# A decoder trunk's first norm: x read a second time by tokens for its square sums, first weights in three pieces, second pair in own buffers

## The chip, the cores and the metric

One core of a Trainium2 chip runs the whole program in one launch. The metric is the device time of one execution in microseconds (us). Kernel before: median 1245.22 us of 3 runs (1245.1 to 1245.67).

## The reference

A trunk of two layers on x of 512 tokens by 1024 features, all in float32. The first step of the first layer is the only part that the change touches:

```
u = x * rsqrt(mean(x*x, over features) + EPS) * conv_norm_g
a = u @ w_pw1 + b_pw1                       # 1024 -> 2048
c = a[:, :1024] * sigmoid(a[:, 1024:])
c = causal depthwise convolution over 31 tokens + dw_b
c = silu(layer_norm(c)) @ w_pw2 + b_pw2
h = x + c
```

Behind it come a SwiGLU block, a gated input embedding, and a second layer with differential attention.

## The kernel before, in words

Activations lie transposed: features on the 128 partitions, the 512 tokens along the free dimension, so x is eight chunks `h[0..7]` of 128x512. Every float32 operand of a large product is cut into an upper and a lower part of reduced precision (ScalarE casts the upper part, VectorE subtracts it from the original), and a product is three matmuls of 128x512 (`mm3`, L165 to L169): lower by upper, upper by upper, upper by lower.

The first step works in chunks c = 0..7 of the output. Each has two weights of 128x1024, one for the gate and one for the value (a pair): 24 matmuls for each of the two. The per-token factor rsqrt(...) is not applied to the input but to the products: `norm.split` (L215) scales a chunk of x by the gain alone and cuts it; the factor comes as a tile `rb` of 128x512 with the same row on each partition, and VectorE multiplies gate and value by it (L567, L573) when they are read from PSUM. So products can start before the factor is known, but nothing behind them can.

The factor is formed so: the squares of the eight chunks (L317, ScalarE) are summed over the features. Chunks 0, 1 and 2 go alone to TensorE and chunks 3 to 7 are first added by GpSimd into one tile (L319); TensorE sums each over its partitions by four matmuls with a matrix of ones (`columns_sum`, L198). VectorE scales the four columns (L262), GpSimd takes the power -0.5 (L264), VectorE spreads the result on a diagonal (L269), TensorE multiplies it by ones (`spread`, L282), and ScalarE copies it to `rb` (L254).

Weights arrive through two buffers `wraw` by DMAs of SyncE's queue (SP in the profile); upper parts have four buffers `whi`, lower parts four `wlo`, so two pairs are in flight. The first pair, weights w0 (gate) and w1 (value), comes in two halves each, between the loads of x; in this prologue the order on ScalarE and VectorE is written out by hand (L327), everything else is ordered by a scheduler. The second pair, w2 and w3, is loaded by `weight` (L148) when `wraw` is free.

After the products, each chunk goes through the 31 taps of the convolution. Chunks 0, 2, 4 and 7 use VectorE (L496, a multiply-add per tap) and GpSimd (L484); chunk 7 also uses TensorE. Chunks 1, 3, 5 and 6 are "phased": the gated product (L579) is written to DRAM (`pi`, L408), read back rearranged (`C<-pi`, L412), multiplied by tap matrices on TensorE (36 matmuls of 128x128, L445), copied by ScalarE (L453), written to DRAM (`po`, L455) and read back (`B<-po`, L458), and VectorE adds the bias (L463). Where a chunk's TensorE taps stand between the products is fixed by `BETWEEN` and `BEHIND` (L62) and the scheduler. The layer norm behind the taps needs the column sums of all chunks (L198 again), a variance (L631 to L633, L262, L264), a diagonal by ScalarE (L641) and its product (L644); products that depend on nothing there (`factor`, L598) fill TensorE meanwhile.

Of the kernel before, what the change touches and what calls it, by code (L numbers as in the profile page):

```python
# [13 lines left out]
F32R = mybir.dt.float32r  # L14
AF = mybir.ActivationFunctionType
ALU = mybir.AluOpType
# [4 lines left out]
P = 128  # L21
S = 512
D = 1024
NC = D // P
# [64 lines left out]


@with_exitstack
def trunk(ctx, tc, xT, pT, wts, diag, dww, vec, rel, onehot, lamv, out):
    nc = tc.nc
    V, A, G, T = nc.vector, nc.scalar, nc.gpsimd, nc.tensor

# [98 lines left out]
    def columns_sum(t, src, first, last):  # L194

        for b in range(4):
            cut = slice(b * P, (b + 1) * P)
            r = T.matmul(t[:, cut], src[:, cut], ones, start=first and b == 0, stop=last and b == 3)  # L198
        return r

    def first_of(t):
        return t.rearrange("p (b k) -> p b k", b=4)[:, :, 0]
# [5 lines left out]
    class Norm:  # L208
# [51 lines left out]
    def rsqrt_cols(src, n, inv):  # L260
        v = sb([P, P // 2], "v8", 2)[:, :8]
        last_v[0] = V.tensor_scalar(v[:, :n], src, inv, EPS, ALU.mult, ALU.add)  # L262
        r = sb([P, P // 2], "r8", 2)[:, :8]
        last_pow[0] = G.tensor_tensor(r[:, :n], v[:, :n], mhalf[:, :n], ALU.pow)  # L264
        return r[:, :n]
# [21 lines left out]


    norm = Norm("conv_g")
    wnext[0] = 2  # L290
    raw2 = [sb([P, 1024], "wraw", 2) for _ in range(2)]
    w0, w1 = ([sb([P, 1024], t, 4, F32R) for t in ("whi", "wlo")] for _ in range(2))
    pieces = ((slice(0, S), slice(S, 1024)),) * 2

    def load(c):
        nc.sync.dma_start(h[c], xT[c])

    def fetch(i, k):
        return nc.sync.dma_start(raw2[i][:, pieces[i][k]], wts[i, :, pieces[i][k]])

    fetch(0, 0)
    load(0)
    load(1)
    fetch(1, 0)
    load(2)
    fetch(0, 1)
    load(3)
    pair_loads = [fetch(1, 1)]
    pairs = [(w1, w0)]
    for c in range(4, NC):  # L310
        load(c)

    squares = {}

    def square(c):
        sq = squares[c] = wk() if c != 3 else sb([P, S], "acc", 1)
        A.activation(sq, h[c], AF.Square)  # L317
        if c > 3:
            G.tensor_tensor(squares[3], squares[3], sq, ALU.add)  # L319

    def first_split(i, k):
        hi, lo = (w0, w1)[i]
        cut = pieces[i][k]
        A.copy(hi[:, cut], raw2[i][:, cut])
        V.tensor_tensor(lo[:, cut], raw2[i][:, cut], f(hi[:, cut]), ALU.subtract)

    with tc.manual_schedule(engines={V.engine, A.engine}):  # L327
        first_split(0, 0)
        norm.split(0)
        square(0)  # L330
        norm.split(1)
        first_split(1, 0)
        norm.split(2)
        first_split(0, 1)
        norm.split(3)
        first_split(1, 1)
        square(1)
        norm.split(4)
        square(3)
        for c in (5, 6, 7):  # L340
            norm.split(c)
            square(c - 1)
        square(7)
        square(2)

    def pfeatures(layer, parts):
        for k, (hi, lo) in enumerate(parts):
# [26 lines left out]
    last_sum = [None]  # L374
    rb = None

    def half(w, behind=None, start=0):
        acc = mm()
        for k in range(NC):
            with tc.issue_after(behind.ins) if behind and k >= start else nullcontext():  # L380
                mm3(acc, wpart(w, k), norm.u[k], k == 0, k == NC - 1)
        return acc

    def wt(c, j):
# [153 lines left out]
    for c in range(NC):  # L538
        wa, wg = pairs[c]
        if c == 0:  # L540
            pg, pa = mm(), mm()
            for k in range(NC):
                mm3(pg, wpart(wg, k), norm.u[k], k == 0, k == NC - 1)
                (ah, al), (bh, bl) = wpart(wa, k), norm.u[k]
                T.matmul(pa, ah, bh, start=k == 0, stop=False)
                T.matmul(pa, ah, bl, start=False, stop=False)
                T.matmul(pa, al, bh, start=False, stop=k == NC - 1)
            norm.dg = diagonal(norm.columns_of_chunks(squares))
            rb = norm.rows()
        if c + 1 < NC:  # L550
            late = ((first_gate, None), (first_gate, last_rows[0])) if c == 1 else ((None, None),) * 2
            pairs.append(tuple(weight(after=i) for i in late)[::-1])
            pair_loads.append(loaded[0])
        if c == 0:
            dwt = sb([P, NC * KW], "C4", 2)
            nc.sync.dma_start(dwt, dww)
        if c == 1:
            ph = pfeatures(0, [(sb([P, S], t, 2, F32R), sb([P, S], t, 2, F32R)) for t in ("wth", "wtl")])
        if c > 0:
            pg = half(wg, last_spread[0] if c == 1 else None, 6)  # L560
            for k in BETWEEN[c]:
                pe_taps(k)
            pa = half(wa, last_spread[0] if c == 1 else None)
# [12 lines left out]
        if c in PHASED:  # L576
            up = big()
            phases, tok = "p (r n) -> p n r", "p (n r) -> p n r"
            V.scalar_tensor_tensor(  # L579
                up.rearrange(phases, r=NPH), ta.rearrange(tok, r=NPH), col("b_pw1", c),  # L580
                tg.rearrange(tok, r=NPH), ALU.add, ALU.mult,
            )
# [771 lines left out]
def _layout(a):  # L1354
# [61 lines left out]
    def chunks(v):  # L1416
# [9 lines left out]
    cols = [chunks(vecs[n]) for n in VEC]  # L1426
    return {
        "xT": a["x"][0].T.reshape(NC, P, S),
        "pT": a["p"][:, 0].transpose(0, 2, 1).reshape(2, 2, P, S).transpose(0, 2, 1, 3).reshape(2, P, 2 * S),
        "wts": np.stack(tiles),  # L1430
        "diag": diag,
# [24 lines left out]
```

## Time and profile before

| | us |
|---|---|
| median of 3 runs | 1245.22 |
| the profiled execution, its own time | 1245.23 |
| its span in the profile | 1243.4 |
| TensorE matmul busy in the span | 1232.1 |
| VectorE, ScalarE, GpSimd busy | 882.0, 624.1, 469.8 |

The span begins with the first recorded instruction and lies 1.83 us below the execution's own time. Busy time of TensorE is modelled and overlaps from one matmul to the next, so small waits don't show in it; where matmuls start is the better reading. All times in rows are counted from the span's start. In a timeline row stand start, length, engine, line, operation, output and inputs, count, and in brackets the idle time before it and what ended it. PE is TensorE, PEld its weight load, DVE VectorE, ACT ScalarE, POOL GpSimd, SP SyncE, and SPq and ACTq are their queues that issue DMAs. A row of a stretch gives the stretch, its length, each engine's busy time, the granted clock, the DMA engines' share and GB/s. "in_wts" are weights, "in_xT" is x by features.

### The profile page before, as it was taken

How to read it: one execution, taken by the hardware profiler on the slowest of the kernel's cores; microseconds unless marked ns; L12 is line 12 of the kernel's file. 1: busy time of each engine (PE TensorE's matmuls, PEld its weight loads, DVE VectorE, ACT ScalarE, POOL GpSimd, SP SyncE). 2: the span in 40 equal slices, each digit the busy share in tenths (PEclk: the TensorE clock that was granted, in tenths of full speed). 3: DMA queues.
4: the chain of work that ended last, by engine and by line, in shares of the span. 5: the costliest groups of instructions: out<-in, count | busy, mean ns of one | idle time of the engine just before them, and what ended most of it. 6: DMA issues, size and time to landing. Idle time of an engine off the chain costs nothing.

```text
span 1243.4 us, 18433 instructions
## 1 busy us (share of the span) xinstructions
PE 1232.1 (99%) x7080; PEld 1080.6 (87%) x7080; DVE 882.0 (71%) x1242; ACT 624.1 (50%) x1096; POOL 469.8 (38%) x355
## 2 busy tenths in 40 slices
PE   9999999999999999999999999999999999999998
PEld 7888788888998899888888888788889998999887
DVE  6997866985895489547676876647966885588535
ACT  6652464433553255435566877735434552455432
POOL 2863432024670464133436635041026650562220
PEclk9999999999999999999999999999999999999999
DMA  7666224234333322334432330142332333232321
GB/s 255 199 212 187 85 55 125 88 99 126 88 100 119 103 86 77 110 104 153 127 111 76 107 101 28 52 152 86 90 126 91 102 114 111 82 103 89 102 99 68
DMA packets 49155, 136.34 MB, mean 110 GB/s; under 512 B 5635, under 2 KB 10243, under 8 KB 49068
## 3 DMA queue, kind: packets, MB, share of 16 engines
q1 hardware_dynamic: 46944, 131.74, 34.2%
q10 hardware_dynamic: 2124, 3.43, 1.0%
q8 instruction: 55, 0.90, 0.3%
q14 instruction: 32, 0.26, 0.1%
HBM read 128.84 MB, written 6.31 MB: 109 GB/s over the span
## 4 chain that ended last, share of the span: by engine, by line
PE 85%; DVE 7%; DMA 3%; issue 2%; ACT 1%; POOL 1%; SPq 1%; DVEq 0%; ACTq 0%; POOLq 0%
PE mm L167 27%; PE mm L168 27%; PE mm L169 27%; DVE sc L496 3%; PE mm L1172 1%; DVE wlo L162 1%; PE sc L1140 1%; PE sc L1139 1%; PE tp L1159 1%; PE tp L1093 1%; DMA B<-po 1%; DMA h<-in_xT 0%; PE tp L198 0%; DMA pi<-big 0%; DMA C<-pi 0%
## 5 line engine op out<-in xcount | busy, mean ns | idle before, releaser
L160 ACT CAST whi<-wraw 128x1024 fp32r<-128x1024 f32 (+1 forms) x141 | 143.5, 1025 | 232.0 <-PE mm L169 115.2
L162 DVE TENSOR_TENSOR wlo<-wraw,whi 128x1024 fp32r<-128x1024 f32 (+1 forms) x137 | 179.3, 1315 | 81.4 <-ACT whi L160 81.0
L167 PE MATMUL mm<-A,wlo 128*128 128x512 f32 (+1 forms) x560 | 218.0, 389 | 0.1
L168 PE MATMUL mm<-A,whi 128*128 128x512 f32 (+1 forms) x560 | 216.7, 387 | 0.0
L169 PE MATMUL mm<-A,whi 128*128 128x512 f32 (+1 forms) x560 | 213.3, 387 | 0.0
L167 PE MATMUL mm<-B,wlo 128*128 128x512 f32 x352 | 137.0, 389 | 0.0
L168 PE MATMUL mm<-B,whi 128*128 128x512 f32 x352 | 137.0, 389 | 0.0
L169 PE MATMUL mm<-B,whi 128*128 128x512 f32 x352 | 135.6, 389 | 0.0
L228 POOL TENSOR_TENSOR acc<-acc,wk 128x512 f32<-128x512 f32 x35 | 60.4, 1726 | 191.2 <-ACT wk L227 190.6
L168 PE MATMUL mm<-C,whi 128*128 128x256 f32 x448 | 126.8, 283 | 0.0
L169 PE MATMUL mm<-C,whi 128*128 128x256 f32 x448 | 126.8, 283 | 0.0
L167 PE MATMUL mm<-C,wlo 128*128 128x256 f32 x448 | 126.8, 283 | 0.0
L167 PEld LDWEIGHTS mm<-A,wlo 128*128 128x128 f32 x560 | 105.2, 188 | 22.1 <-DVE h L1303 0.5
L168 PEld LDWEIGHTS mm<-A,whi 128*128 128x128 f32 x560 | 105.2, 188 | 21.2 <-issue 0.5
L169 PEld LDWEIGHTS mm<-A,whi 128*128 128x128 f32 x560 | 105.2, 188 | 21.0
L766 DVE TENSOR_TENSOR wlo<-A,whi 128x1024 fp32r<-128x1024 f32 x60 | 108.2, 1814 | 19.3 <-ACT whi L765 19.3
L765 ACT CAST whi<-A 128x1024 fp32r<-128x1024 f32 x60 | 62.9, 1048 | 55.1 <-PE mm L169 44.0
L775 POOL TENSOR_TENSOR A<-wraw 128x512 f32<-128x512 f32 x16 | 25.1, 1569 | 168.5 <-DMA wraw<-in_wts 147.2
L775 POOL TENSOR_TENSOR A<-A 128x512 f32<-128x512 f32 x16 | 25.1, 1571 | 164.5 <-DMA A<-in_wts 155.6
L168 PEld LDWEIGHTS mm<-C,whi 128*128 128x128 f32 x448 | 86.0, 192 | 0.2
L167 PEld LDWEIGHTS mm<-C,wlo 128*128 128x128 f32 x448 | 86.0, 192 | 0.2
L169 PEld LDWEIGHTS mm<-C,whi 128*128 128x128 f32 x448 | 86.0, 192 | 0.0
(322 smaller groups left out, 3045.3 us busy)
## 6 DMA issues: line engine op xcount, KB each, us to landing
wraw<-in_wts SPq DMA_DIRECT2D x161, 512.0 KB, 3.6
A<-in_wts SPq DMA_DIRECT2D x32, 512.0 KB, 3.6
wraw<-in_wts SPq DMA_DIRECT2D x16, 384.0 KB, 3.1
D<-in_diag SPq DMA_DIRECT2D x22, 256.0 KB, 5.4
C<-in_diag SPq DMA_DIRECT2D x16, 256.0 KB, 5.1
h<-in_xT SPq DMA_DIRECT2D x8, 256.0 KB, 5.6
rest<-h SPq DMA_DIRECT2D x8, 256.0 KB, 3.0
bias<-scr ACTq DMA_DIRECT2D x8, 256.0 KB, 3.6
```

Source lines behind the costliest of these rows:

```text
L160: A.copy(hi[:, cut], raw[:, cut])
L162: eng.tensor_tensor(lo[:, cut], raw[:, cut], f(hi[:, cut]), ALU.subtract)
L167: T.matmul(acc, al, bh, start=first, stop=False, **kw)
L168: T.matmul(acc, ah, bh, start=False, stop=False, **kw)
L169: return T.matmul(acc, ah, bl, start=False, stop=last, **kw)
L228: self.last = self.eng.tensor_tensor(self.acc, self.acc, sq, ALU.add)
L496: last_v_tap[0] = V.scalar_tensor_tensor(sum_, tap(j), wt(c, j), sum_, ALU.mult, ALU.add)
L765: A.copy(hi, src)
L766: V.tensor_tensor(lo, src, f(hi), ALU.subtract)
L775: G.tensor_tensor(s[:, 0], r1[:, 0], r1[:, 1], ALU.add)
L1093: T.transpose(t[:, i * P : (i + 1) * P], q[:, i * P : (i + 1) * P], ident)
L1139: T.matmul(acc[:, :n], qs[c][:, i, cut], ks[c][:, i, 0:n], start=True, stop=False)
```

## The change

x comes in a second time as `xtok`, by tokens: four blocks of 128 tokens by 1024 features, 512 KB each. ScalarE squares a block in place with an accumulated output, which gives the four columns of sums; the squares by chunks, GpSimd's four additions and TensorE's 32 column matmuls are gone. The blocks lie in the tiles B4 to B7, which later hold convolution results. w2 and w3 get own raw buffers (B2, B3) and are loaded whole. w0 and w1 come in three pieces (256, 256 and 512 columns); w1's first piece is issued from ScalarE's queue. SyncE's order in the prologue, and TensorE's for the first two pairs, is now written out by hand. The factor's spread stands behind the first three matmuls of the second value product. The casts of the third pair (w4, w5) both stand behind `rb`.

```diff
-        def columns_of_chunks(self, squares):
-            t = tp()
-            for c in range(4):
-                columns_sum(t, squares[c], c == 0, c == 3)
-            return rsqrt_cols(first_of(t), 4, 1.0 / D)
+        def factors_of(self, sums):
+            self.dg = diagonal(rsqrt_cols(sums, 4, 1.0 / D))
...
+    raws = [sb([P, 1024], "wraw", 2) for _ in range(2)] + [sb([P, 1024], f"B{i}", 1) for i in (2, 3)]
+    pieces = slice(0, HT), slice(HT, S), slice(S, 1024)
+    fetch(1, pieces[0], nc.scalar)
+    tokens_in = [sb([P, 2, S], f"B{4 + b}", 1) for b in range(4)]
+    with tc.manual_schedule(engines={nc.sync.engine}):
+        fetch(0, pieces[0])
+        load(0)
+        load(1)
+        fetch(0, pieces[1])
+        fetch(1, pieces[1])
+        load(2)
+        load(3)
+        fetch(0, pieces[2])
+        pair_loads = [fetch(1, pieces[2])]
+        for c in range(4, NC):
+            load(c)
+        fetch(2, whole)
+        load_tokens(0)
+        load_tokens(1)
+        pair_loads.append(fetch(3, whole))
+        load_tokens(2)
+        load_tokens(3)
+        dwt = sb([P, NC * KW], "C4", 2)
+        nc.sync.dma_start(dwt, dww)
...
+    def square(b):
+        t = tokens_in[b]
+        A.activation(t, t, AF.Square, accum_out=sums_x[:, b : b + 1])
...
+        for c in range(4, NC):
+            norm.split(c)
+        first_split(2, whole)
         square(0)
-        norm.split(1)
-        first_split(1, 0)
...
         square(1)
-        norm.split(4)
+        first_split(3, whole)
+        square(2)
         square(3)
+        norm.factors_of(sums_x)
...
+            with tc.manual_schedule(engines={T.engine}):
+                pg, pa = mm(), mm()
+                for k in range(NC):
+                    mm3(pg, wpart(wg, k), norm.u[k], k == 0, k == NC - 1)
+                    late_rest(pa, wa, k)
+                g1, a1 = half(pairs[1][1]), mm()
+                for k in range(NC):
+                    late_rest(a1, pairs[1][0], k)
+                    if k == 0:
+                        rb = norm.rows()
+        if 0 < c < NC - 1:
+            late = ((first_gate, last_rows[0]),) * 2 if c == 1 else ((None, None),) * 2
```

What this moves is seen at three places. First TensorE's order around the factor, before: column sums (tp_220) from two tiles of squares stand among the second gate's products (mm_293), and the spread (tp_244) behind 66 matmuls of 128x512.

```order
L198 MATMUL tp_220<-ones_70,wk_165 128x128 x4
L167 MATMUL mm_293<-A_21_117,wlo_249 128x512
L198 MATMUL tp_220<-ones_70,acc_142 128x128 x4
L168 MATMUL mm_293<-A_21_117,whi_248 128x512
L169 MATMUL mm_293<-A_21_117,whi_248 128x512
...
L169 MATMUL mm_293<-A_29_144,whi_248 128x512
L282 MATMUL tp_244<-wk_241,ones_70 128x512
L167 MATMUL mm_293<-A_31_150,wlo_249 128x512
```

The same place in the changed kernel, with mm_244 the second gate and mm_269 the second value:

```order
L168 MATMUL mm_244<-A_40_172,whi_103 128x512
L169 MATMUL mm_244<-A_40_172,whi_103 128x512
L555 MATMUL mm_269<-A_33_141,whi_105 128x512
L556 MATMUL mm_269<-A_33_141,whi_105 128x512
L557 MATMUL mm_269<-A_33_141,wlo_106 128x512
L279 MATMUL tp_274<-wk_187,ones_70 128x512
L555 MATMUL mm_269<-A_34_146,whi_105 128x512
```

The column sums are gone and the spread stands behind 75 matmuls of 128x512 in place of 66. The second place is TensorE at chunk 5's taps (sc_1015 before), with the last gate product of chunk 7 (mm_1097) in front of them:

```order
L167 MATMUL mm_1097<-A_25_132,wlo_955 128x512
L168 MATMUL mm_1097<-A_25_132,whi_954 128x512
L169 MATMUL mm_1097<-A_25_132,whi_954 128x512
L167 MATMUL mm_1097<-A_27_139,wlo_955 128x512
L445 MATMUL sc_1015<-C_166_879,D_191_1016 128x128 x4
L445 MATMUL sc_1015<-C_166_879,D_192_1018 128x128 x4
L445 MATMUL sc_1015<-C_166_879,D_193_1020 128x128
```

And in the changed kernel (taps sc_1003, gate of chunk 7 mm_1085):

```order
L169 MATMUL mm_1085<-A_33_141,whi_942 128x512
L167 MATMUL mm_1085<-A_34_146,wlo_943 128x512
L168 MATMUL mm_1085<-A_34_146,whi_942 128x512
L457 MATMUL sc_1003<-C_162_867,D_187_1004 128x128 x4
L457 MATMUL sc_1003<-C_162_867,D_188_1006 128x128 x4
L457 MATMUL sc_1003<-C_162_867,D_189_1008 128x128
```

Five matmuls of chunk 7's gate stand in front of the taps in place of 13: the taps moved forward by eight. On VectorE the product that these taps read (L579 of chunk 5) has 41 taps and 11 subtractions of weights between the first use of `rb` and itself, in place of 44 and 12. Chunk 1's taps, too, moved forward on TensorE: 20 of the 36 now stand directly behind chunk 2's 48 matmuls, ahead of chunk 3's gate. The third place is ScalarE at the copy of chunk 5's taps, before:

```order
L524 ACTIVATE wk_1093<-B_168_889 128x512
L160 CAST whi_1230<-wraw_1229 128x1024
L524 ACTIVATE wk_1219<-B_180_927 128x512
L453 COPY big_1083<-sc_1015 128x512
L455 DMA po_1085<-big_1083 128x512
L160 CAST whi_1459<-wraw_1458 128x1024
```

And in the changed kernel:

```order
L536 ACTIVATE wk_1081<-B_164_877 128x512
L160 CAST whi_1218<-wraw_1217 128x1024
L465 COPY big_1071<-sc_1003 128x512
L467 DMA po_1073<-big_1071 128x512
L536 ACTIVATE wk_1207<-B_176_915 128x512
L160 CAST whi_1447<-wraw_1446 128x1024
```

The square of chunk 4 (wk_1219 before, wk_1207 now), which waits for VectorE's taps of chunk 4, stood ahead of the copy and now stands behind it. From the taps of chunk 7 on, all five engines have the same order as before.

More of the change, by code (lines that the diff above doesn't have):

```diff
@@ L91, in trunk @@
 @with_exitstack
-def trunk(ctx, tc, xT, pT, wts, diag, dww, vec, rel, onehot, lamv, out):
+def trunk(ctx, tc, xT, xtok, pT, wts, diag, dww, vec, rel, onehot, lamv, out):
     nc = tc.nc
@@ L289, in trunk @@
     norm = Norm("conv_g")
[L290 to L293, printed above, removed]
+    wnext[0] = 4
+    raws = [sb([P, 1024], "wraw", 2) for _ in range(2)] + [sb([P, 1024], f"B{i}", 1) for i in (2, 3)]
+    first = [tuple(sb([P, 1024], t, 4, F32R) for t in ("whi", "wlo")) for _ in range(4)]
+    pieces = slice(0, HT), slice(HT, S), slice(S, 1024)
@@ L295, in load @@
+    whole = slice(0, 1024)
     def load(c):
         nc.sync.dma_start(h[c], xT[c])
[L298 to L325, printed above, removed]
+    def fetch(i, cut, eng=nc.sync):
+        return eng.dma_start(raws[i][:, cut], wts[i, :, cut])
+    fetch(1, pieces[0], nc.scalar)
+    tokens_in = [sb([P, 2, S], f"B{4 + b}", 1) for b in range(4)]
+    def load_tokens(b):
+        nc.sync.dma_start(tokens_in[b], xtok[b].rearrange("p (j k) -> p j k", j=2))
@@ L375, in trunk, with half @@
     rb = None
-    def half(w, behind=None, start=0):
+    def half(w):
         acc = mm()
         for k in range(NC):
-            with tc.issue_after(behind.ins) if behind and k >= start else nullcontext():
-                mm3(acc, wpart(w, k), norm.u[k], k == 0, k == NC - 1)
+            mm3(acc, wpart(w, k), norm.u[k], k == 0, k == NC - 1)
         return acc
```

49 lines of the change are left out of this document (23 added, 26 removed).

## The prediction

> **What bounds the kernel now.** I read the page first, then the stretches of the first 25 us, then the timeline there and at the end of the convolution, then the waits.
>
> ```profile
> PE 1232.1 (99%) x7080; PEld 1080.6 (87%) x7080; DVE 882.0 (71%) x1242; ACT 624.1 (50%) x1096; POOL 469.8 (38%) x355
> PE 85%; DVE 7%; DMA 3%; issue 2%; ACT 1%; POOL 1%; SPq 1%; DVEq 0%; ACTq 0%; POOLq 0%
> ```
>
> TensorE is busy all the time and holds 85% of the chain that ended last; the order of all engines is unchanged from chunk 7's taps on. So a microsecond that TensorE gains before about 155 us should reach the end whole, and only the first 155 us need working out. The first of them:
>
> ```profile
> 5.20 0.50 PE L167 MATMUL mm<-A,wlo 128*128 128x512 f32 x1
> 7.37 0.62 ACT L324 CAST whi<-wraw 128x512 fp32r<-128x512 f32 x1 [1.09 <-DMA wraw<-in_wts]
> 7.98 0.72 ACT L205 ACTIVATE A<-h,vec 128x512 fp32r<-128x512 f32 x1
> 20.47 1.16 PE L198 MATMUL tp<-ones,acc 128*128 128x128 f32 x8 [0.28 <-POOL acc L319]
> 21.66 0.16 DVE L262 TENSOR_SCALAR v<-tp 128x4 f32<-128x4 f32 x1 [0.17 <-PE tp L198]
> 21.90 1.02 POOL L264 TENSOR_TENSOR r<-v,mhalf 128x4 f32<-128x4 f32 x1 [1.49 <-DVE v L262]
> 22.96 0.69 DVE L269 TENSOR_TENSOR wk<-ident,r 128x512 f32<-128x512 f32 x1 [1.14 <-POOL r L264]
> 25.37 1.02 PE L282 MATMUL tp<-wk,ones 128*128 128x512 f32 x2
> 26.43 0.59 ACT L254 COPY rb<-tp 128x512 f32<-128x512 f32 x1 [1.41 <-PE tp L282]
> 26.46 0.40 PE L168 MATMUL mm<-A,whi 128*128 128x512 f32 x1
> 28.25 1.22 DVE L162 TENSOR_TENSOR wlo<-wraw,whi 128x1024 fp32r<-128x1024 f32 x1
> 33.08 0.39 PE L167 MATMUL mm<-A,wlo 128*128 128x512 f32 x1
> ```
>
> Products start at 5.20, the spread at 25.37, chunk 2 at 33.08. From the second product behind the spread (26.46) to chunk 2 are 29 matmuls: 6.62 / 29 = 0.228 us each, the pace of a TensorE that waits for nothing. By the order 66 products stand before the spread: 15.05 us. They took 20.17. The other 5.1 us are the column sums and waits, for w1 at 7.4 and for GpSimd's sum at 20.5. The spread itself costs 26.46 - 25.37 - 0.23 = 0.86.
>
> **The first pair.** x2 is ScalarE's work at 7.98, behind a cast that waited for w1. In the changed queue as many bytes stand before and with x2 (four pieces of 128 KB and three chunks of 256 KB, 1.25 MB, as before two halves and three chunks). So I leave x2 at 7.98, and its upper part at 8.70; the smaller first pieces can bring the start at 5.20 forward, but the next stop is x2 anyway. By then the 12 products of chunks 0 and 1 (2.7 us) are done. From 8.70 on stand 36 of the first pair, 24 of the second gate and three more before the spread: 63 x 0.228 = 14.4, TensorE is there at 23.1. Chunk 7 of x and w2's parts must keep ahead of that (needed at 15.5 and 16.9); they are worth nothing as long as they do.
>
> **The factor** now waits for the last token block. Bytes through it: 3.15 MB as before for x and the first pair, 1.05 for w2 and w3, 2.10 for the tokens, 0.05 for vec: 6.35 MB.
>
> ```profile
> 0.00:7.00 7.00, 5.49 (x30) 5.19 (x31) 2.83 (x9) 3.76 (x5) 0.96 (x10) 1.00 0.70 216
> 7.00:11.00 4.00, 3.54 (x16) 2.51 (x15) 3.02 (x6) 3.56 (x6) 0.00 (x0) 1.00 1.04 400
> 11.00:17.00 6.00, 6.00 (x31) 5.05 (x30) 4.91 (x6) 6.00 (x11) 3.39 (x3) 1.00 0.93 322
> 17.00:21.00 4.00, 3.72 (x24) 3.08 (x23) 4.00 (x3) 1.57 (x3) 3.33 (x2) 1.00 1.05 395
> 21.00:25.00 4.00, 4.00 (x22) 3.37 (x21) 1.35 (x3) 1.03 (x1) 1.02 (x1) 1.00 0.87 285
> SPq L156 <- DVE wlo L325: 2.4, 2, 1.5
> 23.97 1.05 ACT L160 CAST whi<-wraw 128x1024 fp32r<-128x1024 f32 x1 [5.40 <-DMA wraw<-in_wts]
> ```
>
> The last number is GB/s: 1.51 MB by 7, 3.11 by 11, 5.04 by 17, 6.62 by 21 us. On this curve 6.35 MB are through at 20.3. But its dip from 11 to 17 holds SyncE's waits for `wraw` (2.4 us), which own buffers take away; at 400 from 7 us on it is 19.1; at 322 from 11 on, 21.1. From bytes to use: w4, at the end of 7.26 MB (x, two pairs, dww, nine tap matrices, itself; 23.2 on the curve), was cast at 23.97, so 0.7 more; w1, at the end of 1.1 MB (5.1), at 7.37, so 2.3 more. The bounds are 19.8 and 23.4; I take 20.4, the middle of 400 and the curve with w4's 0.7, since these are blocks of the same size late in a full queue. The Trainium skill (HBM Reference, Specifications) gives about 358 GB/s effective per core, and more for a core that streams alone; by 358 from 7 us on the bytes are through at 20.5 in place of 19.1, and the trace's 400 speaks for the lone core.
>
> ```profile
> L160 ACT CAST whi<-wraw 128x1024 fp32r<-128x1024 f32 x3 | 3.1, 1040 | 5.4 <-DMA wraw<-in_wts 5.4
> L317 ACT ACTIVATE wk<-h 128x512 f32<-128x512 f32 x7 | 4.2, 619 | 0.0
> L324 ACT CAST whi<-wraw 128x512 fp32r<-128x512 f32 x4 | 2.5, 620 | 2.3 <-DMA wraw<-in_wts 2.3
> L1190 ACT ACTIVATION_READ_ACCUMULATOR wk<-D x32: 186/190/202, 661.0 to 809.9; 128x1 f32 x32
> ```
>
> A square costs what a cast costs (619, 620 ns at 512), so 1.04 at 1024, and reading the sum 0.19: the last ends at 20.4 + 1.23 = 21.6. The four squares (4.9) replace eight (4.95) on ScalarE, which keeps up with a block each 1.3 us. From the scaling to the diagonal's end it takes 23.65 - 21.66 = 2.0 as before: the spread can start at 23.7. TensorE waits 0.6 there. Behind it 0.86 and 21 products, 4.8: chunk 2 starts at 29.4, **3.7 earlier** than 33.08. `rb` follows the spread's start by 1.65 as before (27.02 - 25.37): 25.4, 1.6 earlier, which is VectorE's gain. w4's lower part ended 2.45 behind `rb` in the trace (28.25 + 1.22); now one more read of PSUM (about 0.7) stands before it: 28.6, in time for 29.4. Behind the waiting spread stand only products; behind the last square ScalarE has `rb`'s copy and the casts of w4 and w5, which come behind the factor anyway. On SyncE's queue w4, w5 and chunk 1's tap matrices (2.36 MB) now stand behind 2.10 MB of tokens: w5 ends 7.53 MB, which at 395 behind 19.7 are through at 22.7, before its cast near 26.5, and the matrices at 28.7, before 40.
>
> **Whether TensorE keeps 3.7.** Its fixed order can meet data that come from VectorE, which gained only 1.6: the phased chunks.
>
> ```profile
> 34.61 1.70 DVE L579 SCALAR_TENSOR_TENSOR big<-big,vec,big 128x512 f32<-128x512 f32 x1
> 39.05 2.01 SPq L412 DMA_DIRECT2D C<-pi  x4
> 99.03 1.16 DVE L579 SCALAR_TENSOR_TENSOR big<-big,vec,big 128x512 f32<-128x512 f32 x1
> 103.69 1.73 SPq L412 DMA_DIRECT2D C<-pi  x4
> 107.42 4.18 PE L445 MATMUL sc<-C,D 128*128 128x128 f32 x36
> C<-pi SPq DMA_DIRECT2D x16, 64.0 KB, 3.8
> B<-po SPq DMA_DIRECT2D x16, 64.0 KB, 2.0
> L496 DVE SCALAR_TENSOR_TENSOR sc<-C,C,sc 128x512 f32<-128x512 f32 x73 | 54.9, 753 | 1.7
> L162 DVE TENSOR_TENSOR wlo<-wraw,whi 128x1024 fp32r<-128x1024 f32 x18 | 29.6, 1651 | 0.7 <-ACT whi L160 0.7
> ```
>
> Chunk 5: taps at 107.42 in the trace, eight products earlier in the new order, so TensorE is there at 107.42 - 1.82 - 3.7 = 101.9. The product they read has three taps (0.75) and one subtraction (1.65) less before it: 99.03 - 3.9 - 1.6 = 93.5. From product to data it took at most 107.42 - 99.03 = 8.4, so they are there at 101.9 or earlier. Chunk 1: TensorE is there at 29.4 + 48 x 0.228 = 40.3; its product ended 9.3 behind `rb` (36.31 - 27.02), with two taps more before it than now (1.5), so it ends at 33.2; to the last issue it took 41.06 - 36.31 = 4.75 in the trace, and a landing of 2.0 to 3.8 makes 40.0 to 41.8. Both meet almost exactly. I charge 0.4 for the two together, with bounds 0 and 1.4.
>
> **The end of the convolution.**
>
> ```profile
> 117.29 0.57 ACT L453 COPY big<-sc 128x512 f32<-128x512 f32 x1
> 126.74 1.12 DVE L463 SCALAR_TENSOR_TENSOR B<-B,vec,shrow 128x512 f32<-128x512 f32 x1 [7.88 <-DMA B<-po]
> 146.84 2.35 DVE L162 TENSOR_TENSOR wlo<-wraw,whi 128x1024 fp32r<-128x1024 f32 x2
> 147.97 1.06 PE L198 MATMUL tp<-ones,wk 128*128 128x128 f32 x8
> 149.57 0.16 DVE L633 SCALAR_TENSOR_TENSOR v<-tp,v 128x4 f32<-128x4 f32 x1
> 153.32 1.12 PE L644 MATMUL tp<-wk,ones 128*128 128x512 f32 x2 [1.18 <-ACT wk L641]
> ```
>
> VectorE idles 7.9 us for chunk 5's return before it starts chunk 7. The taps end 5.5 earlier (1.8 and 3.7), and the copy no longer stands behind a square that waits for VectorE: the return comes about 5 earlier, limited by TensorE's chunk 7. So VectorE has slack at the end, and its two subtractions at 146.84 are done early. Then the variance starts at the column sums' end, 149.03, not at 149.57, and of the 1.18 that TensorE waits for the diagonal 0.5 goes.
>
> **Sum**, against the profiled execution's 1245.23 (span 1243.4, and 1.83 around it; the median is 1245.22): -3.7 + 0.4 - 0.5 = -3.8, so **1241.4**. What a measurement of this kernel can tell from no change is 0.2%, 2.5 us.
>
> **The rivals.**
>
> 1. A slow stream: rates like 322 and the long way to use. The token block is used at 22 to 23.4 and TensorE waits at the spread 1.6 to 3 us longer; the phased chunks then hide it, so 1242.7 to 1244.3, say 1243.5. For it speak 322 and 285 GB/s in stretches with weights; against it 395 and 400 where nothing waits.
>
> 2. Small pieces: each of the four 128 KB pieces costs as much as a half did, 0.65 more (256 KB at 400), so x2 comes 2.6 later; the wait at the spread (0.6) and the ties (0.4) take some of it: 1241.4 + 1.6 = 1243.0. Against it: the DMA engines' share was 1.04 from 7 to 11, so transfers overlap and what a small one costs more is little of it. The Trainium skill (DMA: Bandwidth & Descriptors, Rules for kernel authors) asks for transfers of 1 MB and more and calls those under 64 KB mostly overhead; the pieces lie between.
>
> 3. VectorE's gain is the bound: if both returns are late by their difference, TensorE keeps 1.6 to 2.1 and gets the 0.5: 1242.8.
>
> 4. Slower: chunk 5's taps stand eight matmuls earlier, and TensorE cannot pass them. If the returned data came when they did before, at 107.4, TensorE would start the taps there with 1.82 us less done: 1245.2 + 1.8, less the 0.5 of the end: 1246.5. It decides from 105.6 on; I have 101.9, so `C<-pi` or `pi` must be 3.7 us slower. A queue of tap matrices and weights ahead of them could do that.
>
> **How the numbers follow.** Forecast 57% (its own range 1240.4 to 1242.7), rival 1 20%, rival 2 6%, rival 3 10%, rival 4 7%. The range takes in the forecast's bounds (no wait at the spread: 1240.8; no charge for the ties: 1240.4) and rivals 1 to 3: 1240.4 to 1244.3. Faster by over 0.2% (below 1242.74): 57% and some of rival 3, 60%; within it 33%; slower 7%.
>
> **What would show it.** Right: the last square ends near 21.6, the spread starts near 23.7, chunk 2's products near 29.4, chunk 5's taps near 102, L463 of chunk 5 near 122, the layer norm's spread near 149.5. Wrong: a wait of TensorE over 2 us at the spread, or gaps ahead of the phased taps; or a shift that shrinks behind 155 us, which would make the first step wrong.

## The result, and the profile after

The changed kernel takes 1248.21 us (median of 22 runs, 1246.12 to 1249.96) against 1245.20 (22 runs, 1243.63 to 1246.64): a ratio of 1.0024, with a 95% interval of 1.0018 to 1.0030. It is slower by 3 us, and the prediction had 1241.4 with a range to 1244.3. The first profile of it is from the low end of these runs: span 1244.8, own time 1246.65. A second one, taken later (span 1248.0, own time 1249.75), is nearer to most of them, so both are read here.

The first 30 us came as forecast. From the timeline of the changed kernel: the last square and the read of its sum, the spread, `rb` and chunk 2's first product.

```profile
20.21 1.06 ACT L331 ACTIVATE B<-B 128x1024 f32<-128x1024 f32 x1
21.18 0.18 ACT L331 ACTIVATION_READ_ACCUMULATOR B<-B 128x1 f32 x1
23.45 1.13 PE L279 MATMUL tp<-wk,ones 128*128 128x512 f32 x2
24.62 0.59 ACT L251 COPY rb<-tp 128x512 f32<-128x512 f32 x1 [3.26 <-PE tp L279]
29.23 0.39 PE L167 MATMUL mm<-A,wlo 128*128 128x512 f32 x1
```

The last square ends at 21.4 (forecast 21.6), the spread starts at 23.45 with no wait (23.7, with a wait of 0.6), `rb` is 1.8 us earlier (1.6), chunk 2 3.85 (3.7). That the spread's time fits is in part luck: TensorE got there 0.35 later than forecast, just when the diagonal was done. TensorE also reaches chunk 5's taps as forecast (101.9), at 101.56 + 0.23 = 101.79. There it stops. The timeline of the first profile, from chunk 5's product over SyncE's queue to the taps and the layer norm's spread, with two rows of TensorE's last taps:

```profile
95.24 1.43 DVE L595 SCALAR_TENSOR_TENSOR big<-big,vec,big 128x512 f32<-128x512 f32 x1
96.69 0.33 SPq L420 DMA_DIRECT2D pi<-big  x1
98.79 0.33 SPq L156 DMA_DIRECT2D wraw<-in_wts  x1
99.21 0.86 SPq L470 DMA_DIRECT2D B<-po  x2
100.16 1.80 SPq L424 DMA_DIRECT2D C<-pi  x4
101.56 0.39 PE L168 MATMUL mm<-A,whi 128*128 128x512 f32 x1
104.90 5.81 PE L457 MATMUL sc<-C,D 128*128 128x128 f32 x36 [2.95 <-DMA C<-pi]
114.35 0.39 PE L457 MATMUL sc<-C,D 128*128 128x128 f32 x2
153.60 1.12 PE L660 MATMUL tp<-wk,ones 128*128 128x512 f32 x2 [0.69 <-ACT wk L657]
```

And the same from the second profile, with chunk 3's product and the return of chunk 1 ahead:

```profile
62.48 1.96 DVE L595 SCALAR_TENSOR_TENSOR big<-big,vec,big 128x512 f32<-128x512 f32 x1
74.11 1.14 DVE L475 SCALAR_TENSOR_TENSOR B<-B,vec,shrow 128x512 f32<-128x512 f32 x1 [2.46 <-DMA B<-po]
96.94 1.42 DVE L595 SCALAR_TENSOR_TENSOR big<-big,vec,big 128x512 f32<-128x512 f32 x1
107.60 6.45 PE L457 MATMUL sc<-C,D 128*128 128x128 f32 x36 [5.81 <-DMA C<-pi]
117.69 0.39 PE L457 MATMUL sc<-C,D 128*128 128x128 f32 x2
156.94 1.12 PE L660 MATMUL tp<-wk,ones 128*128 128x512 f32 x2 [0.69 <-ACT wk L657]
```

In the kernel before the last taps stood here:

```profile
115.23 0.39 PE L445 MATMUL sc<-C,D 128*128 128x128 f32 x2
```

Counted from where TensorE's next product could have started (101.79, and 101.63 in the second profile; the rows' 2.95 and 5.81 count from the modelled end of the last one), it waits 3.1 us in the one profile and 6.0 in the other for the data that the prediction had there "at 101.9 or earlier". And then the taps themselves are slow: from the first to the last pair they take 9.45 and 10.09 us, against 115.23 - 107.42 = 7.81 before. The stretches of 2 us (the third number from the end is the granted clock), first the one profile, then the other:

```profile
104.00:106.00 2.00, 1.10 (x5) 1.13 (x6) 0.86 (x2) 0.00 (x0) 0.00 (x0) 0.69 0.72 162
106.00:108.00 2.00, 2.00 (x11) 2.00 (x11) 1.97 (x4) 1.57 (x2) 1.55 (x2) 0.50 0.33 133
108.00:110.00 2.00, 2.00 (x20) 2.00 (x19) 2.00 (x4) 0.00 (x0) 0.96 (x1) 0.96 0.41 131
```

```profile
104.00:106.00 2.00, 0.00 (x0) 0.00 (x0) 1.74 (x2) 0.04 (x1) 0.00 (x0) 0.85 1.11 160
...
110.00:112.00 2.00, 2.00 (x12) 2.00 (x10) 2.00 (x4) 0.56 (x1) 1.61 (x2) 0.50 0.53 131
112.00:114.00 2.00, 2.00 (x18) 2.00 (x18) 2.00 (x3) 0.00 (x0) 0.00 (x0) 0.95 0.23 89
```

A mean of 0.69 from 104 to 106 is half the clock from 104.8 on, 3.0 us after TensorE stopped; in the second profile it is 3.8 (0.85: from 105.4 on). Full speed is back at 108.2 and 112.2, 3.3 and 4.6 us after TensorE had work again. The account in TensorE's order closes at the spread of the layer norm: -3.85 (chunk 2), +3.1 (wait), +1.6 (clock), -0.5 (the spread waits 0.69, not 1.18) make +0.4, and the spread starts 153.60 - 153.32 = 0.3 later than before. In the second profile, where chunk 2 starts at 29.07, it is -4.0 + 6.0 + 2.3 - 0.5 = +3.8, and the spread starts 3.6 later. This tells where the time went; what it would be without one of the terms is another matter (see E3). Behind the spread 1.1 and 1.0 us more are lost.

The runs bear this out: 15 of the 22 have a mean granted clock of 0.996 or 0.997 and take 1248.0 to 1250.0; the other seven (0.998 to 1.000) take 1246.1 to 1248.0.

### The profile page after: what moved, and what is told of

Same layout as the page of the kernel before. It is cut to its first block, busy times and chain, and to the rows that moved or that the text cites. A ratio compares the mean times of both kernels' runs of the same rounds, so it can differ in the third digit from the quotient of the medians.

```text
span 1244.8 us, 18364 instructions
## 1 busy us (share of the span) xinstructions
PE 1231.8 (99%) x7048; PEld 1078.6 (87%) x7048; DVE 879.8 (71%) x1244; ACT 623.7 (50%) x1098; POOL 464.7 (37%) x351
## 4 chain that ended last, share of the span: by engine, by line
PE 84%; DVE 7%; issue 4%; ACT 2%; POOL 2%; DMA 1%; SPq 0%; DVEq 0%; POOLq 0%; ACTq 0%
PE mm L167 26%; PE mm L168 25%; PE mm L169 25%; DVE wlo L782 2%; POOL wk L496 1%; PE mm L1188 1%; DVE sc L508 1%; DVE wlo L162 1%; PE sc L457 1%; PE sc L1155 1%; PE sc L1156 1%; DVE B L873 1%; PE mm L457 1%; PE tp L1175 1%; PE tp L1109 1%
## 5 line engine op out<-in xcount | busy, mean ns | idle before, releaser
L160 ACT CAST whi<-wraw 128x1024 fp32r<-128x1024 f32 (+1 forms) x139 | 141.2, 1024 | 219.8 <-PE mm L169 110.3
L162 DVE TENSOR_TENSOR wlo<-wraw,whi 128x1024 fp32r<-128x1024 f32 (+1 forms) x135 | 174.2, 1296 | 81.9 <-ACT whi L160 81.1
L167 PE MATMUL mm<-A,wlo 128*128 128x512 f32 (+1 forms) x552 | 214.0, 388 | 0.1
L168 PE MATMUL mm<-A,whi 128*128 128x512 f32 (+1 forms) x552 | 213.4, 387 | 0.0
L169 PE MATMUL mm<-A,whi 128*128 128x512 f32 (+1 forms) x552 | 211.0, 388 | 0.0
L169 PEld LDWEIGHTS mm<-A,whi 128*128 128x128 f32 x552 | 103.6, 188 | 22.3 <-DVE A L206 1.1
L168 PEld LDWEIGHTS mm<-A,whi 128*128 128x128 f32 x552 | 103.8, 188 | 20.5
L782 DVE TENSOR_TENSOR wlo<-A,whi 128x1024 fp32r<-128x1024 f32 x60 | 107.5, 1802 | 19.7 <-ACT whi L781 19.7
L791 POOL TENSOR_TENSOR A<-wraw 128x512 f32<-128x512 f32 x16 | 23.7, 1482 | 169.8 <-DMA wraw<-in_wts 147.0
```

Source lines behind the costliest of these rows:

```text
L160: A.copy(hi[:, cut], raw[:, cut])
L162: eng.tensor_tensor(lo[:, cut], raw[:, cut], f(hi[:, cut]), ALU.subtract)
L167: T.matmul(acc, al, bh, start=first, stop=False, **kw)
L168: T.matmul(acc, ah, bh, start=False, stop=False, **kw)
L169: return T.matmul(acc, ah, bl, start=False, stop=last, **kw)
L782: V.tensor_tensor(lo, src, f(hi), ALU.subtract)
```

## The experiments

### Is it the place of the taps?

My first theory (A) was the prediction's rival 4 with a clock on top: the taps stand too early, so TensorE waits and cools. Four kernels went with it on one chip (the kernel before there: 1245.58).

**E1**: the taps behind 18 products of chunk 7's gate, not 5.

```diff
+            if c == NC - 2:
+                g7 = half(pairs[NC - 1][1], None, range(6))
+            with tc.issue_after(last_gate[0].ins) if c == NC - 2 else nullcontext():
                 for k in BEHIND[c]:
                     pe_taps(k)
```

> The changed kernel with chunk 5's taps held behind 18 of the 24 products of chunk 7's gate instead of 5; nothing is left out. Theory A (the loss is made at these taps: TensorE waits 3.1 us there, and the lower clock behind the wait costs 1.6 more): 13 products, 3.0 us, fill the wait, the 36 taps take 8.0 us instead of 9.6, the granted clock stays at 1.00 from 104 to 110, and the time is 3 to 4 us below the kernel before (1241 to 1242). Rival B (the loss comes from elsewhere, such as the 2.1 MB more that are read, or it comes back in the later stages): 1 to 3 us above the kernel before, as the changed kernel. Rival C (VectorE, which gained only 1.6, is the bound): the wait turns up at the returns of chunks 5 to 7 or at the layer norm, 1 to 2 us below the kernel before.

Measured: 1249.12 (ratio to the kernel before 1.0032, 95% interval 1.0020 to 1.0045; so in brackets from here on). The clock stayed at 1.00, and nothing was gained: 3.5 us above the kernel before, half a microsecond beyond rival B's range, and with rival C's waits. TensorE's waits in E1 from 5 to 160 us (total, times, longest):

```profile
PE mm L415 <- issue: 2.2, 1, 2.2
PE tp L665 <- ACT wk L662: 1.2, 1, 1.2
PE sc L198 <- DVE acc L545: 1.1, 1, 1.1
PE sc L459 <- DMA C<-pi: 1.0, 1, 1.0
PE mm L459 <- DVE big L594: 0.9, 1, 0.9
```

The one wait has become five, at the taps of chunks 5, 6 and 7, at the column sums and at the spread. So theory A falls: what TensorE waits for is late as a whole.

**E2**: the kernel before, with chunk 7's gate wholly behind chunk 5's taps.

```diff
-            pg = half(wg, last_spread[0] if c == 1 else None, 6)
+            pg = half(wg, last_spread[0] if c == 1 else last_tap[0] if c == NC - 1 else None, 6 if c == 1 else 0)
```

> The kernel before with one edge more: all products of chunk 7's gate stand behind chunk 5's taps, which so come 13 products (3.0 us) earlier in TensorE's order. Theory A: the data land near 107.4 as before, TensorE is there at 104.4 and waits 3 us, as in the changed kernel; the lower clock adds up to 1.6: 3 to 4.6 us above the kernel before, less up to 0.5 that comes back at the layer norm. Rival B: the place of the taps is not what costs; the scheduler moves other work into the wait, within 1 us of the kernel before.

Measured: 1248.28 (1.0023, 1.0014 to 1.0033), 2.7 above. TensorE waited 3.0 us for `C<-pi` as expected, and the clock fell (0.89 from 100 to 110). So the place does cost, where the data are on time; but E1 says that it isn't what held the changed kernel.

**E3**: 13 useless products in the wait.

```diff
+                t = tp()
+                with tc.issue_after(last_gate[0].ins):
+                    for k in range(13):
+                        last_gate[0] = T.matmul(t[:, 0:P], ident, ones, start=True, stop=True)
```

> The changed kernel with 13 useless 128x128 products (whose sums nobody reads) ahead of chunk 5's taps, behind the sixth product of chunk 7's gate: TensorE does about 3 us of nothing instead of waiting. If the clock behind the wait costs as theory A says: the data still land near 104.9, no clock below 1.00 from 104 to 110, the taps take 8.0 us instead of 9.6, and the time is 1.6 us below the changed kernel. If the wait alone costs: the time of the changed kernel within 0.5 us, and the taps still take over 9 us.

Measured: 1249.03 (1.0032, 1.0020 to 1.0045), the time of the one outcome expected with the fast taps of the other. Chunk 5's taps and the later waits of TensorE in E3:

```profile
107.47 4.26 PE L459 MATMUL sc<-C,D 128*128 128x128 f32 x36 [1.58 <-DMA C<-pi]
PE tp L669 <- ACT wk L666: 1.2, 1, 1.2
PE mm L415 <- POOL acc L545: 1.1, 1, 1.1
PE sc L198 <- DVE acc L545: 1.1, 1, 1.1
```

The data came at 107.5, as in the second profile, the clock stayed at 1.00, and the taps were done 2.3 us sooner than there. Yet the span is the same (1248.2 and 1248.0): the 2.3 are waited out at chunk 7's taps, the column sums and the spread. The low clock is real, but it lay beside something longer.

**E4**: one load moved on SyncE's queue.

```diff
-    pw = [weight(), weight()]
+    pw = [weight(), weight(behind=last_in[5])]
```

> The changed kernel with one load moved on SyncE's queue: the second feature weight (512 KB, issued at 98.79 between chunk 5's write of pi and its four reads) now stands behind those reads; the taps stand one product later. Theory A, with this load as a cause of the late data: the reads start near 99.2 instead of 100.2 and share the DMA engines with no weight, so they land 1.5 to 2.5 us earlier (102.5 to 103.4); TensorE waits 0.5 to 1.5, too short for the clock to fall, and the time is 3 to 4 us below the changed kernel. If the load is not what makes the data late: they land at 104.5 to 105 again, the wait stays near 3 us, and the time is that of the changed kernel.

Measured: 1247.24 (1.0017, 1.0008 to 1.0026), 1.7 above the kernel before where the changed kernel is 3.0 above it: a gain of 1.4 and not of 3 to 4, and as the two intervals overlap it is not clear of the noise. Chunk 5's taps in E4:

```profile
103.95 4.26 PE L461 MATMUL sc<-C,D 128*128 128x128 f32 x36 [1.57 <-DMA C<-pi]
```

The load did make the data late: chunk 5's product came at 97.14, as in the second profile (96.94), and the data were there at 103.95, 6.8 us behind it, in place of 107.60. But here, too, TensorE's later waits grew as its wait at the taps shrank (to 1.6): 1.6 us at chunk 7's taps, 1.1 at the column sums, 1.2 at the spread.

### Is it VectorE?

What is late in all of these is VectorE. The stretches of the kernel before (busy time of PE, PEld, DVE, ACT, POOL), and one of the changed kernel's first profile:

```profile
70.00:80.00 10.00, 10.00 (x46) 8.29 (x45) 9.87 (x14) 3.38 (x5) 1.30 (x1) 1.00 0.41 124
90.00:100.00 10.00, 10.00 (x46) 8.29 (x45) 9.68 (x12) 3.51 (x5) 7.98 (x8) 1.00 0.39 146
```

```profile
70.00:80.00 10.00, 10.00 (x63) 8.91 (x62) 8.35 (x12) 3.44 (x5) 1.67 (x2) 1.00 0.39 109
```

VectorE has no slack in the convolution: 97 to 99% busy in these stretches before. In the changed kernel it stands still for 1.6 us from 70 to 80. The timeline of VectorE, before: chunk 3's product, the taps of chunk 2 behind it, the addition that takes in chunk 1's return.

```profile
64.06 1.47 DVE L579 SCALAR_TENSOR_TENSOR big<-big,vec,big 128x512 f32<-128x512 f32 x1
69.37 2.34 DVE L496 SCALAR_TENSOR_TENSOR sc<-C,C,sc 128x512 f32<-128x512 f32 x3
74.78 1.15 DVE L463 SCALAR_TENSOR_TENSOR B<-B,vec,shrow 128x512 f32<-128x512 f32 x1
```

The same in the changed kernel:

```profile
61.20 1.92 DVE L595 SCALAR_TENSOR_TENSOR big<-big,vec,big 128x512 f32<-128x512 f32 x1
66.99 0.75 DVE L508 SCALAR_TENSOR_TENSOR sc<-C,C,sc 128x512 f32<-128x512 f32 x1
72.37 1.16 DVE L475 SCALAR_TENSOR_TENSOR B<-B,vec,shrow 128x512 f32<-128x512 f32 x1 [1.58 <-DMA B<-po]
```

On SyncE's queue chunk 1's return stands behind chunk 3's write and reads of `pi`, so it comes some 11 us after VectorE starts chunk 3's product, whenever that is: the wait ended 11.2 behind it here and 11.6 in the second profile. Before, 10.72 us of work stood between the two; in the new order one tap stands where three did, 9.59 us of work are left, and VectorE waits. (Counted from the first instruction behind chunk 3's product it is clearer still: 9.42 us of work before, 7.82 now, and the return after 9.40.) Theory V: VectorE is the bound of the whole stretch, and the new order made it spend its lead of 1.8 us (and more, in most runs) on waits. Four kernels on one chip (the kernel before there: 1245.77):

**Six taps fewer** for VectorE, in each kernel (this leaves out taps of chunk 2; in the changed kernel chunk 5's taps also stand one product later):

```diff
-        for j in range(b + 1, KW):
+        for j in range(b + (7 if c == 2 else 1), KW):
```

> The changed kernel with six of chunk 2's taps on VectorE left out (4.5 us of VectorE's work ahead of chunk 5's product; chunk 4's taps are held to their old places, chunk 5's taps stand one product later). Theory V (VectorE's chain through the convolution is the bound; its 1.8 us of lead were spent on waits for returns and casts, and TensorE then waited for it): chunk 5's product comes 3 to 4.5 us earlier, TensorE waits under 1 us at its taps with the clock at 1.00, the 3.7 us of the prologue stay, and the time is 3 to 5 us below the kernel before (1240.5 to 1242.5). Rival B (the loss comes from the tokens' 2.1 MB or in later stages): 1 to 3 us above the kernel before, as the changed kernel, less up to 1 us.

> The kernel before with the same six taps of chunk 2 left out and chunk 4's held to their places. Theory V: TensorE did not wait for VectorE at the phased chunks here, so all that can come is part of the 1.2 us that it waits ahead of the layer norm's spread: 0 to 1.2 us below the kernel before. Were VectorE's work worth as much here as in the changed kernel, it would be 3 us or more below.

Measured: changed 1241.46 (0.9968, 0.9957 to 0.9980), before 1244.12 (0.9989, 0.9981 to 0.9998). The same 4.5 us of VectorE's work are worth 7.3 us in the changed kernel (from 3.0 above the kernel before to 4.3 below it) and 1.65 in the one before. That the first is more than the work left out is not explained by a run of its own; with TensorE's wait the low clock behind it goes too. The last lies 0.45 beyond what I expected. In the changed kernel TensorE then walks through chunk 5's taps without a wait:

```profile
102.19 4.18 PE L460 MATMUL sc<-C,D 128*128 128x128 f32 x36
```

**Both returns three taps later** on VectorE, all work kept:

```diff
+            if late_shift and j == b + {1: 6, 3: 10}[late_shift[0][0]]:
+                with tc.issue_after(last_v_tap[0].ins):
+                    last_shift[0] = late_shift.pop()[1]()
```

> The changed kernel with the additions that take in the returns of chunk 1 and chunk 3 standing three taps later in VectorE's order (behind the sixth and the tenth tap of the next chunk); chunk 5's taps stand one product later. Nothing is left out. Theory V: the waits of 1.6 us (72.4) and 1.1 us (105.2) go, chunk 5's product comes 1 to 2 us earlier less the one or two instructions that now stand ahead of it, TensorE waits 1.5 to 2.5 us at its taps, the clock falls for less time or not at all, and the time is 1.5 to 3 us below the changed kernel. If VectorE's waits are not what counts: the time of the changed kernel within 0.7 us.

Measured: 1242.70 (0.9977, 0.9967 to 0.9986): 3.1 below the kernel before, and so 6.1 better than the changed kernel, twice what I had expected. Its timeline:

```profile
62.48 1.95 DVE L603 SCALAR_TENSOR_TENSOR big<-big,vec,big 128x512 f32<-128x512 f32 x1
74.39 1.14 DVE L477 SCALAR_TENSOR_TENSOR B<-B,vec,shrow 128x512 f32<-128x512 f32 x1
92.68 1.53 DVE L603 SCALAR_TENSOR_TENSOR big<-big,vec,big 128x512 f32<-128x512 f32 x1
102.70 4.26 PE L458 MATMUL sc<-C,D 128*128 128x128 f32 x36 [0.48 <-DMA C<-pi]
149.62 1.12 PE L668 MATMUL tp<-wk,ones 128*128 128x512 f32 x2 [0.69 <-ACT wk L665]
```

Chunk 3's product stands where the second profile has it, 62.48. There is no wait at the return, chunk 5's product comes at 92.68 and not at 96.94, TensorE waits 0.5 and the clock stays. The spread starts 3.7 us earlier than before, at 149.62, where the prediction had named 149.5. The way from chunk 5's product to the data is still 10.0 us, so the gain is VectorE's and not the queue's. From chunk 3's product to chunk 5's VectorE does the same 35 instructions in 30.2 us that took 34.5 there; 2.46 of the 4.3 are the wait, and the rest is in single instructions (see the end).

**All moves together**: both returns later, taps behind 12 products, two loads behind the reads of `pi`, the copy of chunk 5's sums ahead of chunk 4's square.

```diff
+        behind = last_in[{17: 5, 19: 6}[i]] if i in {17: 5, 19: 6} else None
...
+                g7 = half(pairs[NC - 1][1], None, range(4))
...
+        with tc.issue_after(last_factor[0].ins) if c > NC - 3 else tc.issue_after(last_out[0].ins) if c == 4 else nullcontext():
```

> The changed kernel with four moves and nothing left out: both returns later in VectorE's order as in the run just named; chunk 5's taps behind 12 products of chunk 7's gate; the second feature weight behind chunk 5's reads of pi and a weight of the linear stage behind chunk 6's; the square of chunk 4 behind the copy of chunk 5's sums. Theory V: no wait over 0.5 us at chunk 5's taps, clock 1.00, chunk 6's reads land 1 to 2 us earlier and with them chunk 5's return, and the time is 2 to 4 us below the kernel before (1241.5 to 1243.5). Rival B: 1 to 3 us above it.

Measured: 1243.16 (0.9979, 0.9970 to 0.9988); the later returns alone do as much. Chunk 5's taps came at 103.36 without a wait, as expected, but chunk 5's return was late (124.79, against 122.46 with the later returns alone). The profile is of the slowest of its runs (1246.14): TensorE waits 2.0 us at the column sums, and the clock falls there (0.54 from 144 to 146).

### Which wait, and whose?

The last runs (the kernel before there: 1245.90).

**Chunk 1's return alone** later, the dictionary being `{1: 6}`:

> The changed kernel with chunk 1's return alone taken in three taps later on VectorE (chunk 3's stays where it was). Theory V: it is this wait, the first and the longer one, that used up VectorE's lead before chunk 5's product: the wait of 1.6 us at 72.4 goes, chunk 5's product comes near 93, its taps start near 103, and the time is within 0.7 us of the run with both returns later (2.5 to 3.5 us below the kernel before). If both waits share the loss: 0 to 2 us below the kernel before.

Measured: 1243.54 (0.9984, 0.9976 to 0.9993), 2.4 below the kernel before, just short of the 2.5 expected. The first wait is most of the loss: 5.4 of the 6.1 us come back with it. Chunk 5's product came at 91.83, its taps at 102.37. The other wait, for chunk 3's return, lies behind that product (1.9 us here), and TensorE waits 0.7 us at the column sums, which it doesn't with both returns later.

**The kernel before with later returns**, `{1: 8, 3: 12}`, and the taps held at 12 products:

> The kernel before with both returns taken in three taps later on VectorE, and chunk 5's taps held at 12 products of chunk 7's gate (13 before), so that TensorE's order stays. Theory V: VectorE did not wait for either return here, so nothing is gained: within 1 us of the kernel before. If the later returns are worth something by themselves, in whatever kernel: 2 us or more below it, and then the changed kernel's gain in the run with both later would not be the prologue's.

Measured: 1247.29 (1.0013, 1.0004 to 1.0022): 1.4 above the kernel before, not below. So the order that saves the changed kernel is no gain in itself. I had expected no change; it costs a little (chunk 6's product came at 111.97 in place of 108.35).

**One more load moved**, the taps behind nine products:

```diff
+        behind = last_in[{17: 5}[i]] if i in {17: 5} else None
...
+                g7 = half(pairs[NC - 1][1], None, range(3))
```

> The changed kernel with both returns later, the second feature weight behind chunk 5's reads of pi on SyncE's queue, and chunk 5's taps behind nine products of chunk 7's gate in place of six. What is left to gain there is the 0.5 us that TensorE still waits at these taps and part of the 0.7 ahead of the layer norm's spread: 2.5 to 4 us below the kernel before. If VectorE or chunk 5's return takes it back, as in the run with 18 products: the same as the run with both returns later or up to 1 us slower.

Measured: 1242.65 (0.9980, 0.9970 to 0.9989), 3.3 below, the same as with both returns later. The wait at the taps went (they start at 102.51), but the one ahead of the spread is 1.2 us again. These two versions lie 0.2% below the kernel before and 0.4 to 0.5% below the changed one.

**The changed kernel again**:

> The changed kernel once more, for a second profile. Its time has a wide spread (1246.1 to 1250.0), and the profile seen so far is from its fast end. Theory V: a run of 1248 to 1250 has VectorE 1 to 2 us later at chunk 3's product than that profile (62.5 to 63 in place of 61.2), chunk 5's data land at 106 or later, TensorE waits 4 us or more there and the clock is low for longer. If the spread is made elsewhere: VectorE and the taps stand as in the first profile, and the difference shows in a later stage.

Measured: one run of 1249.75; its profile is the second one above. All of it stands as expected: chunk 3's product at 62.48, data at 107.60, 6.0 us of wait, and half the clock for 6.8 us (105.4 to 112.2) in place of 3.4 (104.8 to 108.2). It is one run, but its time and its mean clock (0.996) are those of most of the 22.

## Why the prediction was wrong

**The prologue** was right: each of its times came within 0.3 us, and `rb` 1.8 us earlier (1.6).

**The step that failed** is "Whether TensorE keeps 3.7", in the line on chunk 5: "three taps (0.75) and one subtraction (1.65) less before it: 99.03 - 3.9 - 1.6 = 93.5 ... they are there at 101.9 or earlier", charged with 0.4 and bounds of 0 and 1.4 for both ties. Three things in it were wrong.

1. The product came at 95.24 and 96.94, not at 93.5. I counted the instructions that the new order takes away ahead of it, and carried VectorE's 1.6 us along as if nothing could stop it. But the same order had taken two taps out from between chunk 3's product and chunk 1's return. Those two were the cover of that return. VectorE waits 1.58 and 2.46 us there. With the return moved back behind three taps the product came at 91.8 to 92.7, so without the wait the 93.5 was no bad estimate.

2. From the product to the data it was 9.7 and 10.7 us, not "at most 8.4". The new order on SyncE's queue puts a weight load of 512 KB behind the write of `pi` and ahead of its reads (98.79); before, a load was issued ahead of the write (99.13, the write at 100.21). The reads were issued 3.5 us behind the write in both kernels (before, four reads of `po` stood between). What grew is the time from the last read's issue to the taps: 2.9 and 4.0 us, before at most 2.0. With the load behind the reads (E4) product to data took 6.8 us.

3. Nothing in the sum had a price for the clock behind a wait. Rival 4 told this wait almost as it came, but had 7%, decided "from 105.6 on", and priced it with 1.82 us of products undone; its 1246.5 is about what the first profile shows (1246.65), but by luck: it has the data at 107.4 and no low clock, where the profile has them at 104.9, 1.6 us of low clock and 1.1 lost behind 155 us. In the second profile the data came at 107.6, and the taps took 2.3 us more at the low clock.

Rival 3 ("VectorE's gain is the bound") had the right engine. It lacked the thought that a bound can move: VectorE, at 97 to 99% busy, did not keep its 1.6 us; its product for chunk 5 came 1.7 and 3.4 us behind the forecast. Chunk 1's taps, the other tie, came without any wait (40.1, forecast 40.3). The end of the convolution gave its 0.5, but not in the way forecast: chunk 5's return came at 126.15 and not near 122 (the last section shows what its write waited for), and VectorE's two subtractions started at 147.07, no earlier than before (146.84). The column sums came 0.8 us later, so that the variance could start at their end.

What stays open: the 1 us lost behind 155 us. The prediction named a shift that shrinks there as the sign that its first step ("should reach the end whole") is wrong, and by this much it is. In ten profiles of the changed kernel and its variants the span grew 0.2 to 1.3 us behind the spread, in three variants of the kernel before -0.5 to 0.3. Part of it has a place: near 1122 us, where TensorE's products wait for VectorE's `big`, the ten lose 0.4 to 0.7 us and the three 0.1 to 0.3. Why `big` is late there, and where the rest goes, is not known. Nor was it tried why VectorE reaches chunk 3's product 1.3 us later in one run than in the next.

On the clock, gaps of TensorE of 1.6 us (E3, E4) left it at 1.00, and those of 3.0 (E2), 3.1 and 6.0 brought it down to 0.50. Between them it goes either way: E1's gap of 2.2 us left it at 1.00, and one of 2.1 us in the run with all moves (141.7 to 143.9) brought it down. The Trainium skill (TensorE: Matmul & The Clock Gate, Why this matters for your kernels) asks for no gaps of TensorE over about 3 us; the long gaps agree, the one of 2.1 us shows that staying below 3 was not enough here. In the changed kernel the low clock took no time of its own, though, as E3 shows: VectorE was later still.

## What to carry to other kernels

When a scheduler orders anew behind a faster start, look on the busiest engine beside TensorE at what used to stand between a result and its return over a queue: an order that takes two instructions out from there turns them into a wait, and the engine has no slack to make it good. Before a wait of TensorE is repaired where it shows, ask whether what comes behind it is late too: here filling the wait, keeping the clock and shortening the queue gave 0 to 1.4 us, and two instructions moved on VectorE gave 6. And a gap on TensorE is priced with the low clock behind it (1.6 us more for 3.1 here, 2.3 for 6.0), but that price counts only if what comes next is ready.

## What the runs showed that I had not expected

The same subtraction on VectorE takes 1.2 us or 2.3. Two rows of VectorE in the changed kernel, and one of GpSimd in the same stretch:

```profile
76.15 1.22 DVE L162 TENSOR_TENSOR wlo<-wraw,whi 128x1024 fp32r<-128x1024 f32 x1
82.37 2.34 DVE L162 TENSOR_TENSOR wlo<-wraw,whi 128x1024 fp32r<-128x1024 f32 x1
```

```profile
79.64 8.96 POOL L496 TENSOR_TENSOR wk<-wk,C 128x512 f32<-128x512 f32 x6 [4.06 <-ACT C L495]
```

From 75.6 to 79.6 GpSimd stood still and the subtraction took 1.22; the other ran beside its additions. In the two kernels all subtractions up to 155 us that met no GpSimd work took 1.21 to 1.23; those that met it, 1.2 to 2.34. Meeting it is not enough, then: one at 41.08 ran beside GpSimd's additions almost throughout and took 1.23. A shift of GpSimd's work by a microsecond may so change VectorE's pace; that this makes the spread between runs is a guess that no run tried.

And chunk 5's return could not start when its sums were copied. The copy and the write of `po`, first in the changed kernel, then in E4:

```profile
114.77 0.58 ACT L465 COPY big<-sc 128x512 f32<-128x512 f32 x1 [6.86 <-PE sc L457]
118.58 0.33 ACTq L467 DMA_DIRECT2D po<-big  x1
```

```profile
112.26 0.59 ACT L469 COPY big<-sc 128x512 f32<-128x512 f32 x1 [3.68 <-PE sc L461]
118.99 0.33 ACTq L471 DMA_DIRECT2D po<-big  x1
```

The transfers' completions are counted on eight semaphores in turn, and the program has the write wait for the transfer that last used its own. By the order that is a read of chunk 6's `pi`:

```
94 L424 DMA C_197_1065<-pi_1063 32x4x128 [waits DMAHW2_49]
91 L467 DMA po_1073<-big_1071 128x512 [waits DMAHW2_49,Activation_49]
```

The first row is SyncE's, the second ScalarE's. Those reads were issued from 112.1 on, the one in question at 112.5, and the transfers of that stretch list a median of 6.0 us to landing for them: 118.5, and the write is issued at 118.58. So the return of chunk 5 hangs from chunk 6's product on VectorE, though its own sums were copied 3.2 and 6.1 us sooner; E4's taps came 2.5 us earlier, and the write of `po` no earlier. In the kernel before the copy ended at 117.86 and the write was issued at 118.44, so the prediction's "about 5 earlier" for this return needed chunk 6's reads to come earlier as well; with both returns later on VectorE they did, and the return came at 122.46. That this wait is what kept E4 and E1 from gaining is argued from these rows, not tried.
